# Batch norm after a matmul: six y blocks transposed raw by DMA, one store held to the end, and another warm-up on zeros

## The chip, the cores and the metric

One core of one Trainium2 chip runs the kernel. The metric is device time in microseconds (us) from launch to end; the profile's span, from the first to the last instruction, is somewhat shorter. The kernel before takes 207.84 us, the median of 8 runs (207.38 to 209.17).

## The reference

```python
y = np.matmul(x, weight)                     # x: 16 x 512 x 1024, weight: 1024 x 768, float32
mean = np.mean(y, axis=(0, 1), keepdims=True)
var = np.var(y, axis=(0, 1), keepdims=True)
y_norm = (y - mean) / np.sqrt(var + eps)
return (gamma * y_norm + beta).astype(np.float32)
```

So there are M = 8192 rows, K = 1024 and N = 768 columns. Every column is normalised with the mean and the variance of its 8192 values, so no value of a column can be stored before the whole column has been computed.

## The kernel before, in words

**Tiling.** The rows are cut into 16 chunks of 512 (c = 0 to 15), the columns into six tiles of 128 (nt = 0 to 5). x and weight are cast to bf16 by the loading DMAs, which POOL issues (L392, L383). DVE transposes x in 32 x 32 blocks (L421, L414) into `xT_sb`. Some chunks are copied once more into a plain layout `x_pl` (L530), on ACT during the loads; for chunks 11 to 15 the copies are made late, on POOL or DVE.

**Two ways to compute y.** The first two column tiles (256 columns) are computed with rows on the partitions for the first 14 chunks (L493) while x arrives; their sums lie in `sum1`, `sum2`, `sum3`. Column tiles 2 to 5 are computed with columns on the partitions (L558), so that statistics are one `bn_stats` on each bank (L694) and y is then cast to bf16 into `y_sb` tiles (L698). A y block is two chunks of one column tile: 128 columns by 1024 rows. After the last chunk of a column tile come its `bn_aggr` (L960), a root on ACT (L974) and the four small DVE operations of `affine` (L977 to L981), which give scale and shift.

**Ways out for a y block.** The block has to be transposed, normalised, widened to float32 and stored.
- `pe`: DVE normalises it (L1010), TensorE transposes it in eight 128 x 128 steps (L1028, through `turn_block`), put one by one between the long matmuls; ACT copies the bank out (L1171), SP stores (L1163).
- `xact`: DVE normalises it (L1010; for nt = 2 ACT does, L1007), SP issues a DMA transpose (L1181), ACT widens it (L1193), SP stores (L1163).
- raw: SP transposes the block by DMA before it is normalised (`raw_turn`, L1090). Scale and shift of that column tile are spread over 128 partitions by two float32 matmuls (`raw_spread`, L887), DVE multiplies (L1135), and one engine adds the shift (L1139), POOL before; SP stores (L1143). All raw transposes wait for the last load and are issued in one run ahead of the first store.

**Before**, raw blocks are c = 0 and 2 of nt = 2 and of nt = 4. The other blocks: nt = 2 has six `xact`, nt = 3 eight `xact`, nt = 4 one `xact` and five `pe`. Column tile 5 comes last: its final pieces (L736), their statistics (L743), `affine` (L1255 to L1257), normalisation (L1280), 64 transposes on TensorE (L1028), copies on ACT (L1293) and eleven stores by SP (L1296).

**Order.** Every engine runs its instructions in the order in which the builder emitted them (`seq`). That order comes from a planner (`arrange`): every task has a due time, a modelled duration for each engine that may do it, and the buffers it takes; the planner simulates the engines and picks. So a change of a mode moves other work too: an `x_pl` copy, which POOL and DVE may both do, goes to whichever the planner finds free. SP issues in order, so an instruction that waits holds everything behind it.

**The head.** While the first loads are under way, `wake` (L570) runs TensorE on a tile of zeros: 8 float32 matmuls of 512 columns (two passes each, 16 instructions, L574) and 22 bf16 matmuls of 128 columns (L577). Four tiny loads of weight values (L345, `touched`) are issued by SP at the start.

**Buffers.** There are 28 `y_sb` tiles (YB), which raw results and late `x_pl` copies share, and a float32 ring for results with room for six blocks, freed when a store has landed.

Of the kernel before, what the change touches and what calls it, by code (L numbers as in the profile page):

```python
# [227 lines left out]
def kernel(  # L228
# [9 lines left out]
    nc = tc.nc  # L238
    f32 = mybir.dt.float32
# [8 lines left out]
    P = 128  # L248
# [4 lines left out]
    C = M // CH  # L253
    QR = 256
    QPC = CH // QR
    JW = KQ // 64
    PIECES = ((0,QR),(QR,QR))
    WAKE = 8
    FILL = 2
    SMALL = 22  # L260
    TOUCH = 1
    EARLY = 4
    SHORT = 2
    GA = 2
    NA = GA * P
    GY = 2
    PAD = 54
    HELD = 0
    ASTAT = {2:tuple(range(4,16))}
    RC = C - 2  # L270
    XT, YB, SQ = C - EARLY, 28, 3
    ADDED = (0,6,16,28,40)
    PARTED, LATE, SINGLE = (4,5,7,8,9,10), (12,13,14,15,11), (2,3,6)
    MODE = {2:'xact',3:'xact',4:('pe',)*2+('xact',)*1+('pe',)*5}
    MODE = {nt: m if isinstance(m, tuple) else (m,) * (C // GY) for nt, m in MODE.items()}
    RAW, RAWADD, RAWDUE = {2:(0,2),4:(0,2)}, {2:'POOL',3:'POOL',4:'POOL'}, {2:14.0,3:8.0,4:8.0}
    RING = 3 * CH // 32 * KQ // 2
    ENG = {"ACT": nc.scalar, "DVE": nc.vector, "POOL": nc.gpsimd, "SP": nc.sync}

# [3 lines left out]
    singles = ctx.enter_context(tc.tile_pool(name="singles", bufs=1))  # L283
# [7 lines left out]
    def seq(bi):  # L291

        ins = bi.ins
        prev = last.get(ins.engine)
        if prev is not None:
            tc.add_manual_dep(
                ins, prev,
                mybir.DependencyInfo(mybir.DependencyClass.NoSync, mybir.DependencyReason.DATA),
                reason="order",
            )  # L300
        last[ins.engine] = ins.name
        return bi
# [12 lines left out]
    ones = singles.tile([P, 1], f32)  # L315
    seq(nc.vector.memset(ones, 1.0 / (RC * CH)))
    ident32 = singles.tile([P, P], f32)
    sum1 = singles.tile([P, 2 * NA], f32)
    sum2 = singles.tile([P, 2 * NA], f32)
    sum3 = singles.tile([P, 2 * NA], f32)  # L320
    for acc in (sum1, sum2, sum3):
        seq(nc.vector.memset(acc, 0.0))
    tot = singles.tile([P, 2, NA], f32)
    stats = singles.tile([P, (NT - GA) * C + PAD, 6], f32)
    fin = singles.tile([P, 9 + 6 * len(PIECES)], f32)
    psums = {nt: singles.tile([P, 2, C], f32, name=f"psums{nt}") for nt in ASTAT}
# [12 lines left out]
    warm = singles.tile([P, 1], f32)  # L339

    seq(nc.scalar.activation(warm, eps_sb, AF.Sqrt))
    touched = singles.tile([P, TOUCH], f32)
    first_rows = weight.rearrange("(i jw c e) n -> i jw c (e n)", i=4, jw=JW, e=2)
    for i in range(4):
        seq(nc.sync.dma_start(touched[32 * i:32 * i + 32], first_rows[i, 0, :, 0:TOUCH]))  # L345


    tasks, turns = [], {}
# [2 lines left out]
    def task(prio, engines, emit, deps=(), lock=False, **kw):  # L351
        t = Task(prio, engines, emit, deps, **kw)
        t.lock = lock
        tasks.append(t)
        return t
# [14 lines left out]
    STORE, XBAR = 1 / 350.0, 1.25  # L370
# [63 lines left out]
    for kind, n, *n1 in order:  # L434
# [13 lines left out]
        slot = Slot(rings, rows // 32 * KQ // 2)  # L448
# [7 lines left out]
        for i in range(rows // QR):  # L456
            c, q = divmod(m0 // QR + i, QPC)
            for j0, j1 in ((0, JW // 2), (JW // 2, JW)) if m0 < CH else ((0, JW),):
# [4 lines left out]
                    uses=[slot] if new else [slot, x_slot[c]], takes=[x_slot[c]] if new else [])  # L463
# [3 lines left out]
        if rows % QR:  # L467
            t0 = rows // QR * QR // 32
            m1 = m0 + 32 * t0
            c, q = divmod(m1 // QR, QPC)  # L470
# [139 lines left out]
    def col_unit(nt, c, jws, q0=0, q1=QPC):  # L610
        slot = bank_of.setdefault((nt, c), None) or Slot(banks)
        bank_of[nt, c] = slot
        first = jws[0] == 0 and q0 == 0
        xs = [plain[c][0][jw] for jw in jws] if c in plain else [x_slot[c]]
        kw = {"takes": [slot], "uses": xs} if first else {"uses": [slot] + xs}
        t = pe_task((1.728 if c in plain or c in SINGLE else 1.808) * len(jws) / JW * (q1 - q0) / QPC,
                    mm(nt, c, list(jws), slot, q0, q1),
                    waits(jws, c, q0, q1) + ([plain[c][1][jw] for jw in jws] if c in plain else []), (nt, c), **kw)
        if q1 - q0 == QPC:
            t.hosts = 4  # L620
        if jws[-1] == JW - 1 and q1 == QPC:
            col_stats(nt, c, slot, t)
        return t
# [60 lines left out]
    col_end = {}  # L684
# [91 lines left out]
    def merge(i):  # L776
        def emit(eng):
            acc = (sum1, sum2)[i]
            seq(ENG[eng].tensor_add(tot[:, i], acc[:, 0:NA], acc[:, NA:2 * NA]))
        return emit  # L780

    def more(h):
        def emit(eng):
            seq(nc.gpsimd.tensor_add(tot[:, 1], tot[:, 1], sum3[:, h * NA:(h + 1) * NA]))
        return emit

    ga_half = {}
# [46 lines left out]
    U = clock[0] - 30.0  # L834
# [14 lines left out]
    def sums_rows(eng):  # L849
        tot_ps = psum.tile([P, CH], f32, tag="b")  # L850
        aff["tot"] = tot_ps
        for i in range(2):
            for a in range(GA):
                j = i * GA + a
                seq(nc.tensor.matmul(  # L855
                    tot_ps[:, j:j + 1], tot[:, i, a * P:(a + 1) * P], ones,
                    start=True, stop=True, skip_group_check=True,
                ))

# [41 lines left out]
    U = S - 30.0  # L901
# [12 lines left out]
    def rows_out(c, s0, s1, k):  # L914
        due = S + 5.0 + 0.62 * k
        n = s1 - s0
        slot = Slot(rings, n * NA)

        def norm(eng):
            slot.o = piece(slot).rearrange("p (s n) -> p s n", n=NA)  # L920
            seq(nc.vector.tensor_mul(  # L921
                slot.o, y_row[c].y[:, s0:s1], aff[0][:, None, :].to_broadcast([P, n, NA])))

        def add(eng):
            row = sum1[:, 0:NA] if eng == "POOL" else aff[1]
            seq(ENG[eng].tensor_add(slot.o, slot.o, row[:, None, :].to_broadcast([P, n, NA])))  # L926

        def store(eng):
            m0 = c * CH
            seq(nc.sync.dma_start(  # L930
                out_flat[m0 + s0 * P:m0 + s1 * P, 0:NA].rearrange("(s p) n -> p s n", p=P), slot.o))

        keeps = [row_end[k][3] for k in row_end if k[0] == c]
        a = task(due, dve(0.3 * n), norm, [p0] + keeps, takes=[slot], uses=[y_row[c], a0_slot])
        b = task(due + 0.4, dve(0.3 * n) if k in ADDED else pool(0.59 * n), add, [a, p1 if k in ADDED else sh],
                 uses=[slot, a1_slot] if k in ADDED else [slot])
        task(due + 1.0, {"SP": (0.38, 0.4)}, store, [b], dma=n * NA * P * 4 / 1024 / 365.0 * 1.024,
             uses=[slot])

    k = 0  # L940
    for c in range(RC):
        for s0_, s1_ in ((0, 2), (2, 4)) if c < 2 else ((0, 4),):
            rows_out(c, s0_, s1_, k)
# [139 lines left out]
    def raw_turn(nt, c):  # L1083

        yslot, slot = y_of(nt, c), Slot(ys)

        def xbar(eng):
            r_sb = ypool.tile([P, GY * RT, P], bf16, tag="y")
            slot.r = r_sb
            bi = nc.sync.dma_start_transpose(slot.r, y(nt, c, GY))  # L1090
            if not gated:
                tc.add_manual_dep(
                    bi.ins, gate.ins.name,
                    mybir.DependencyInfo(mybir.DependencyClass.Sync, mybir.DependencyReason.DATA),
                    reason="behind the loads",
                )
                gated.append(bi)
            seq(bi)

        b = task(U, {"SP": (1.4, 1.4)}, xbar, [col_end[nt, c + i][1] for i in range(GY)] + [gate], dma=XBAR,  # L1100
                 takes=[slot], uses=[yslot])
        raw[nt, c] = slot, b

    raw, gated, raw_aff = {}, [], {}
    gate = last_loads[-1]
    for nt in RAW:
        for c in RAW[nt]:
            raw_turn(nt, c)

    def raw_spread(nt, fin_task):  # L1110
        bank = Slot(banks)
# [96 lines left out]
    for nt in range(GA, NT - 1):  # L1208
        if nt == NT - 2:
            for i, c in enumerate(LATE):  # L1210
                part_chunk(c, clock[0] + 0.0 + 4.0 * i, {"POOL": (1.1, 1.15), "DVE": (0.63, 0.7)},
                           i == 0, 4.0 / 4, [col_end[NT - 3, late[-1]][1]])
        for c in CHUNKS[nt]:
            for jws in halves if nt > GA or c > EARLY + 2 else [[jw] for jw in range(JW)]:
                col_unit(nt, c, jws)
        f = finish_tasks(nt)
        start = clock[0] + 3.0
        if nt in RAW:
            raw_spread(nt, f)
        for i in range(C // GY):  # L1220
            if (nt, GY * i) in raw:
                raw_block(nt, GY * i, start + STEP[nt] * i + RAWDUE[nt])
                continue
            if nt == NT - 2 and C // GY - HELD <= i:
                held.append((nt, GY * i, f))
                continue
            col_block(nt, GY * i, start + STEP[nt] * i, f)


    nt = NT - 1  # L1230
# [35 lines left out]
    for i, (hn, hc, hf) in enumerate(held):  # L1266
        b = col_block(hn, hc, E + 0.3 + 0.3 * i, hf)
# [3 lines left out]
    for c, r0, rows in ends:  # L1271
        due = E + 2.0 + 0.6 * c
        n = max(rows // CH, 1)
# [3 lines left out]
        for i in range(n):  # L1277
            def norm_part(eng, c=c + i, r0=r0, rows=min(rows, CH)):
# [5 lines left out]
                              uses=[y_of(nt, c + i)]))  # L1284
# [3 lines left out]
        slot = Slot(xts)  # L1288
# [6 lines left out]
        def store(eng, slot=slot, m0=m0, count=count):  # L1295
# [6 lines left out]
             uses=[slot])  # L1302
# [41 lines left out]
```

## Time and profile before

| what | us |
|---|---|
| median of 8 runs | 207.84 |
| the profiled execution | 207.81 |
| its span | 205.9 |
| around the span (207.81 less 205.9) | 1.9 |
| TensorE busy | 192.0 (93%) |
| DVE busy | 156.7 (76%) |
| ACT busy | 140.0 (68%) |
| POOL busy | 132.0 (64%) |

How to read it: the chain of work that ended last is followed back from the last instruction to whatever released each step. TensorE instructions are pipelined and overlap, so start-to-start times are read, not the sum of single durations. Loads fill the DMA engines up to 97 us and stores fill them from about 110 us on; between the two lies a stretch of about 10 us in which only the raw transposes run. A DMA queue's row shows when an instruction was issued, and for how long the issuing took, not when the data landed.

### The profile page before, as it was taken

The page shows a single profiled execution, that of the slowest core. Times are in us where ns is not written, and L with a number is a line of the kernel's source. Part 1 is how long each engine was busy: PE and PEld are TensorE (multiplying, and loading weights), DVE is VectorE, ACT ScalarE, POOL GpSimd, SP SyncE. Part 2 cuts the span into 40 slices and gives each one's busy share as a digit, 9 for nine tenths or more (in the row PEclk, how much of TensorE's full clock was granted, in tenths as well). Part 3 has the DMA queues.
Part 4 walks back from the last instruction along what each step waited for, and adds up shares of the span by engine and source line. Part 5 has one row for each costly group of instructions (what it writes and reads, how often), then busy time and mean ns, then how long its engine had stood idle before and what let it go on. Part 6 is the DMA issues. An engine that isn't in the chain of part 4 may idle for free.

```text
span 205.9 us, 3521 instructions
## 1 busy us (share of the span) xinstructions
PE 192.0 (93%) x1226; PEld 116.2 (56%) x1226; DVE 156.7 (76%) x238; ACT 140.0 (68%) x248; POOL 132.0 (64%) x148
## 2 busy tenths in 40 slices
PE   7999999999999999999999999999999999996900
PEld 3466564747488888777875444444444445553600
DVE  4220879998999999968989998888999648947900
ACT  2000560368989999998979767997476776866950
POOL 7877964877498999999304998599945440440000
PEclk9999999999999999999999999999999999999995
DMA  4999999999999999999696898999999999999898
GB/s 48 178 180 194 194 196 196 199 195 197 190 193 197 197 197 196 196 197 195 105 136 200 312 338 294 261 351 288 323 324 251 290 323 325 274 342 347 255 347 246
DMA packets 98497, 48.73 MB, mean 237 GB/s; under 512 B 24240, under 2 KB 97968, under 8 KB 98480
## 3 DMA queue, kind: packets, MB, share of 16 engines
q0 software_dynamic: 34688, 18.36, 65.1%
q1 hardware_dynamic: 63792, 30.16, 53.6%
q8 instruction: 9, 0.15, 0.3%
q14 instruction: 8, 0.07, 0.1%
HBM read 36.71 MB, written 25.17 MB: 300 GB/s over the span
## 4 chain that ended last, share of the span: by engine, by line
PE 82%; DMA 8%; ACT 3%; POOL 1%; issue 1%; DVE 1%; ACTq 0%; POOLq 0%
PE y_ps L558 52%; PE y_ps L493 23%; DMA ring<-in_x_dram 5%; PE y_ps L798 4%; ACT o_sb L1293 3%; DMA w_sb<-in_weight_dram 3%; PE o_ps L1028 2%; PE a_ps L887 1%; POOL ring L392 1%; PE y_ps L736 1%; PE o_ps L1058 0%; ACTq L1339 0%; PE tot_ps L855 0%; DVE fin L743 0%; ACT y_sb L746 0%
## 5 line engine op out<-in xcount | busy, mean ns | idle before, releaser
L558 PEld LDWEIGHTS <-w_sb 128*128 128x128 bf16 x512 | 49.6, 97 | 57.4
L558 PE MATMUL y_ps<-x_pl,w_sb 128*128 128x512 bf16 x264 | 61.3, 379 | 0.0
L558 PE MATMUL y_ps<-xT_sb,w_sb 128*128 128x512 bf16 (+1 forms) x248 | 55.9, 377 | 0.0
L392 POOL DMA_DIRECT2D ring<-in_x_dram x76 | 47.4, 628 | 12.5 <-DVE xT_sb L414 5.0
L493 PE MATMUL y_ps<-w_sb,xT_sb 128*128 128x256 bf16 x448 | 50.5, 273 | 0.3 <-DMA w_sb<-in_weight_dram 0.3
L493 PEld LDWEIGHTS <-xT_sb 128*128 128x128 bf16 x448 | 43.6, 98 | 7.8 <-issue 1.1
L421 DVE STREAM_TRANSPOSE xT_sb<-ring 128x1024 f32<-128x1024 f32 (+1 forms) x29 | 31.2, 1110 | 12.7 <-DMA ring<-in_x_dram 12.6
L694 DVE BATCH_NORM_STATS2 stats<-y_ps 128x6 f32<-128x512 f32 x46 | 30.7, 686 | 11.8 <-PE y_ps L558 11.6
L698 ACT CAST y_sb<-y_ps 128x512 bf16<-128x512 f32 x51 | 29.4, 590 | 14.2 <-DVE stats L694 11.6
L926 POOL TENSOR_TENSOR ring<-ring,sum 128x1024 f32<-128x1024 f32 (+1 forms) x11 | 23.8, 2184 | 14.8 <-DVE ring L921 14.7
L649 POOL TENSOR_TENSOR sum<-sum,sq_sb 128x512 f32<-128x512 f32 x21 | 26.9, 1281 | 2.9 <-ACT sq_sb L642 1.7
L642 ACT ACTIVATE sq_sb<-y_ps 128x512 f32<-128x512 f32 x28 | 16.2, 609 | 17.4 <-PE y_ps L493 17.0
L530 ACT COPY x_pl<-xT_sb 128x1024 bf16<-128x1024 bf16 x24 | 24.4, 1058 | 1.7 <-DVE xT_sb L421 1.7
L645 DVE TENSOR_TENSOR sum<-y_ps,sum 128x512 f32<-128x512 f32 x28 | 18.9, 674 | 8.5 <-ACT sq_sb L642 7.2
L655 ACT CAST y_sb<-y_ps 128x512 bf16<-128x512 f32 x28 | 16.1, 598 | 7.9 <-DVE sum L645 7.6
L530 POOL COPY x_pl<-xT_sb 128x1024 bf16<-128x1024 bf16 x15 | 16.0, 1106 | 8.0 <-DVE x_pl L530 5.2
L921 DVE TENSOR_TENSOR ring<-y_sb,a_ps 128x1024 f32<-128x1024 bf16 (+1 forms) x16 | 16.7, 1079 | 0.8 <-DMA out_dram<-ring 0.8
L1193 ACT CAST ring<-ring 128x1024 f32<-128x1024 bf16 x15 | 15.7, 1049 | 1.5 <-DMA ring<-y_sb 1.5
L1139 POOL TENSOR_TENSOR ring<-ring,sum 128x1024 f32<-128x1024 f32 x4 | 9.7, 2416 | 10.7 <-DVE ring L1135 10.7
L1028 PE MATMUL o_ps<-ident,y_sb 128*128 128x128 bf16 x104 | 14.2, 221 | 2.1 <-DVE y_sb L1280 2.0
L414 DVE STREAM_TRANSPOSE xT_sb<-ring 128x2048 bf16<-128x2048 bf16 x6 | 13.5, 2290 | 0.1
L574 PE MATMUL idle_ps<-idle_sb 128*128 128x512 f32 x20 | 11.2, 715 | 1.5 <-DVE idle_sb L314 1.5
(97 smaller groups left out, 155.2 us busy)
## 6 DMA issues: line engine op xcount, KB each, us to landing
out_dram<-ring SPq DMA_DIRECT2D x38, 512.0 KB, 3.8
ring<-in_x_dram POOLq DMA_DIRECT2D x52, 256.0 KB, 8.9
out_dram<-o_sb SPq DMA_DIRECT2D x6, 512.0 KB, 4.8
ring<-in_x_dram POOLq DMA_DIRECT2D x16, 128.0 KB, 5.3
out_dram<-ring SPq DMA_DIRECT2D x4, 256.0 KB, 3.0
w_sb<-in_weight_dram POOLq DMA_DIRECT2D x8, 96.0 KB, 4.9
w_sb<-in_weight_dram POOLq DMA_DIRECT2D x4, 192.0 KB, 5.6
ring<-in_x_dram POOLq DMA_DIRECT2D x4, 192.0 KB, 8.2
```

What stands on the lines that cost most here:

```text
L392: bi = seq(nc.gpsimd.dma_start(x_bf[32 * i:32 * i + 32], src[:, :, KQ * i:KQ * (i + 1)]))
L421: seq(nc.vector.transpose(dst, src[:, :, jw0:jw1]))
L493: seq(nc.tensor.matmul(y_ps[:, s], x_of(c, jw, e, t * P, (t + 1) * P), w_sb[:, jw, e, 0:NA], start=(s == 0 and jw == 0 and e == 0), stop=( ...
L530: seq(nc.scalar.copy(dst, pairs) if eng == "ACT" else ENG[eng].tensor_copy(dst, pairs))
L558: seq(nc.tensor.matmul(y_ps, w_sb[:, jw, e, nt * P:(nt + 1) * P], moving(c, jw, e, q0 * QR, q1 * QR, parted), start=(jw == 0 and e == 0 an ...
L645: seq(nc.vector.tensor_add(sum1, slot.tile[:, 0:n], sum1))
L649: seq(ENG[eng].tensor_add(acc, acc, state["sq"][:, 0:n]))
L694: seq(nc.vector.bn_stats(dst, slot.tile))
L698: seq(nc.scalar.copy(y(nt, c), slot.tile))
L921: seq(nc.vector.tensor_mul(slot.o, y_row[c].y[:, s0:s1], aff[0][:, None, :].to_broadcast([P, n, NA])))
L926: seq(ENG[eng].tensor_add(slot.o, slot.o, row[:, None, :].to_broadcast([P, n, NA])))
L1028: seq(nc.tensor.transpose(dst, src, ident))
```

## The change

- The raw blocks become six: c = 0 and 2 of nt = 2, 3 and 4. Their shift is added by DVE, not by POOL. `raw_spread` runs for nt = 3 too.
- nt = 3 has six `xact` blocks then (two fewer); nt = 4 has three `xact` (two more) and three `pe` (two fewer). One of the three `pe` blocks is held (HELD = 1): its transposes, its copy and its store come after the last long matmul, ahead of column tile 5's own.
- `wake` runs 5 float32 matmuls (10 instructions) and 72 small ones.
- The four tiny loads (`touched`) are left out.
- The row sums are folded in place in `sum1` and `sum2`, so the tile `tot` goes; the statistics tile is padded by less; there is one more `y_sb` tile (29).
- Of the 20 late `x_pl` copies POOL makes 19 and DVE one; before it was 15 and 5. This follows from the planner.

```diff
-    WAKE = 8
+    WAKE = 5
     FILL = 2
-    SMALL = 22
-    TOUCH = 1
+    SMALL = 72
...
-    PAD = 54
-    HELD = 0
+    PAD = 13
+    HELD = 1
...
-    XT, YB, SQ = C - EARLY, 28, 3
+    XT, YB, SQ = C - EARLY, 29, 3
...
-    MODE = {2:'xact',3:'xact',4:('pe',)*2+('xact',)*1+('pe',)*5}
+    MODE = {2:'xact',3:'xact',4:('pe',)*2+('xact',)*3+('pe',)*3}
...
-    RAW, RAWADD, RAWDUE = {2:(0,2),4:(0,2)}, {2:'POOL',3:'POOL',4:'POOL'}, {2:14.0,3:8.0,4:8.0}
+    RAWBEHIND = {}
+    RAW, RAWADD, RAWDUE = {2:(0,2),3:(0,2),4:(0,2)}, {2:'DVE',3:'DVE',4:'DVE'}, {2:14.0,3:0.0,4:0.0}
...
-    tot = singles.tile([P, 2, NA], f32)
...
-    touched = singles.tile([P, TOUCH], f32)
-    first_rows = weight.rearrange("(i jw c e) n -> i jw c (e n)", i=4, jw=JW, e=2)
-    for i in range(4):
-        seq(nc.sync.dma_start(touched[32 * i:32 * i + 32], first_rows[i, 0, :, 0:TOUCH]))
...
-            seq(ENG[eng].tensor_add(tot[:, i], acc[:, 0:NA], acc[:, NA:2 * NA]))
+            seq(ENG[eng].tensor_add(acc[:, 0:NA], acc[:, 0:NA], acc[:, NA:2 * NA]))
...
-            seq(nc.gpsimd.tensor_add(tot[:, 1], tot[:, 1], sum3[:, h * NA:(h + 1) * NA]))
+            seq(nc.gpsimd.tensor_add(sum2[:, 0:NA], sum2[:, 0:NA], sum3[:, h * NA:(h + 1) * NA]))
```

The rest of the diff only names things: `RAWBEHIND` is empty and adds no wait, and the loops over raw blocks give the same order for these blocks.

More of the change, by code (lines that the diff above doesn't have):

```diff
@@ L855, in sums_rows @@
                 seq(nc.tensor.matmul(
-                    tot_ps[:, j:j + 1], tot[:, i, a * P:(a + 1) * P], ones,
+                    tot_ps[:, j:j + 1], (sum1, sum2)[i][:, a * P:(a + 1) * P], ones,
                     start=True, stop=True, skip_group_check=True,
@@ L936, in rows_out @@
                  uses=[slot, a1_slot] if k in ADDED else [slot])
-        task(due + 1.0, {"SP": (0.38, 0.4)}, store, [b], dma=n * NA * P * 4 / 1024 / 365.0 * 1.024,
-             uses=[slot])
-    k = 0
+        row_stores.append(task(due + 1.0, {"SP": (0.38, 0.4)}, store, [b],
+                               dma=n * NA * P * 4 / 1024 / 365.0 * 1.024, uses=[slot]))
+    k, row_stores = 0, []
     for c in range(RC):
@@ L1098, in xbar @@
             seq(bi)
-        b = task(U, {"SP": (1.4, 1.4)}, xbar, [col_end[nt, c + i][1] for i in range(GY)] + [gate], dma=XBAR,
+        b = task(U, {"SP": (1.4, 1.4)}, xbar, [col_end[nt, c + i][1] for i in range(GY)] + [gate]
+                 + [row_stores[k] for k in RAWBEHIND.get((nt, c), ())], dma=XBAR,
                  takes=[slot], uses=[yslot])
@@ L1107 @@
         for c in RAW[nt]:
-            raw_turn(nt, c)
+            if c < EARLY:
+                raw_turn(nt, c)
     def raw_spread(nt, fin_task):
@@ L1215 @@
                 col_unit(nt, c, jws)
+        for c in RAW.get(nt, ()):
+            if c >= EARLY:
+                raw_turn(nt, c)
         f = finish_tasks(nt)
```

## The prediction

> **What bounds the kernel now.** I read the chain that ended last first, then its pieces in time.
>
> ```profile
> PE 82%; DMA 8%; ACT 3%; POOL 1%; issue 1%; DVE 1%; ACTq 0%; POOLq 0%
> ```
> ```profile
> 19.38 1.91 PE y_ps L493 x16
> ...
> 174.38 0.06 PE o_ps L1028
> 174.44 0.22 PE y_ps L558
> ...
> 186.49 1.83 PE y_ps L736 x16
> 188.34 0.44 DVE fin L743
> ```
> From 19.38 to 188.3 us TensorE never lets go of the end. Each transpose of a `pe` block (L1028) put between long matmuls costs it 0.055 us, the distance from 174.38 to 174.44. After 188.3 come statistics, then column tile 5's stores. What bounds those is in the stretches of 1 us (columns: busy us of PE, PEld, DVE, ACT, POOL, then clock, DMA share, GB/s).
>
> ```profile
> 190.00:191.00 1.00, 0.62 (x6) 0.31 (x7) 1.00 (x4) 0.34 (x2) 0.00 (x0) 1.00 1.01 307
> 191.00:192.00 1.00, 1.00 (x14) 0.71 (x15) 1.00 (x4) 0.96 (x4) 0.00 (x0) 1.00 0.09 29
> 192.00:193.00 1.00, 1.00 (x15) 0.71 (x14) 1.00 (x4) 1.00 (x2) 0.00 (x0) 1.00 0.87 260
> 203.00:204.00 1.00, 0.00 (x0) 0.00 (x0) 0.00 (x0) 0.00 (x0) 0.00 (x0) 0.50 1.15 347
> ```
> The DMA engines finish the older stores at about 190.8, stand still for 1 us, then move the eleven last stores at 347 GB/s until 204.45 (the next row has 156 GB/s, 0.45 of a full one). So the end is TensorE's end, a chain of small steps, and then bytes over bandwidth.
>
> **What the Trainium skill says.** "TensorE: Matmul & The Clock Gate", section "Wait — 56ns, not 53.3ns?": a warm 128-column matmul follows the last after 55.6 ns, a cold one after about 107 ns. The trace agrees on the first: 22 small ones from 10.63 to about 11.85 us, 0.055 each. "SBUF — State Buffer", section "Who interferes with whom": a DVE instruction in a two-port mode and a GpSimd instruction shut each other out. The trace agrees: the normalisation L1010 takes 0.54 us alone, 1.22 us at 148.66 beside POOL's copies. "DMA: Bandwidth & Descriptors", section "Latency and other measured facts": a DMA transpose (with a strided middle dimension) moved 261 GB/s. The trace is a little better: 284 to 295 GB/s where one runs, 340 to 360 in stores alone.
>
> **The head.**
> ```profile
> 10.63 1.39 PE L577 MATMUL idle_ps<-idle_sb 128*128 128x128 bf16 x22
> ...
> 19.38 1.91 PE L493 MATMUL y_ps<-w_sb,xT_sb 128*128 128x256 bf16 x16 [0.28 <-DMA w_sb<-in_weight_dram]
> ```
> Six long instructions go, at the warm distance of 0.43 us (their weight loads stand at 9.34, 9.77, 10.20): -2.57. Fifty small ones come: 50 x 0.055 = +2.75. The first real matmul moves from 11.86 to about 12.0. The cover: before 19.38 TensorE waits 0.28 us for the last piece of weight. Cost 0; without the cover +0.2. If the clock fell during the zeros, all 72 would take 0.107 (the skill's cold figure): +3.7 us, 3.5 behind the cover. The small ones before ran warm, so I take 0. The four tiny loads: SP does nothing else then; weights issued at 3.73 land 4.8 us later, 8.5 to 10.1, for use at 11.86, so 1.8 us of delay would be free, and no gain is in them, since x itself lands at 8.15. I take 0; up to +1 if weights come much later without them. In-place folding: the same operations, 0.
>
> **Six raw transposes.**
> ```profile
> 100.65 6.92 SPq L1090 DMA_TRANSPOSE r_sb<-y_sb  x4
> 109.61 0.41 SPq L930 DMA_DIRECT2D out_dram<-ring  x1
> ```
> The four were issued at 100.65, 102.08, 103.48 and 106.3, the third and fourth only when the first and second had landed (2.8 and 4.2 us later), since they take buffers that those free. With one more buffer the third needn't wait and the fourth waits for the first; the sixth waits for the third. At 1.4 us each I get an issue end of about 109.0 for six. The first store is ready at 109.58, so nothing moves. Behind SP stand all row stores; if each transpose cost its full 1.4 us, 107.57 + 2.8 = 110.4, +0.8 for them, while the DMA engines still have room (309 to 337 GB/s up to 125 us). I take 0.
>
> **DVE and POOL.**
> ```profile
> L1139 POOL TENSOR_TENSOR ring<-ring,sum 128x1024 f32<-128x1024 f32 x4 | 9.7, 2416 | 10.7 <-DVE ring L1135 10.7
> L1135 DVE TENSOR_TENSOR ring<-r_sb,a_ps 128x1024 f32<-128x1024 bf16 x4 | 4.8, 1209 | 0.1
> L926 DVE TENSOR_TENSOR ring<-ring,a_ps 128x1024 f32<-128x1024 f32 x3 | 3.6, 1214 | 0.1
> ```
> DVE gains six adds, 6 x 1.21 = 7.3, and two multiplies, 2.4; it loses two normalisations (0.67 each) and four copies (0.76 each): +5.3 us. POOL loses 9.7 and gains 4 x 1.1. DVE was busy for 27.0 of the 30 us from 130 to 160, so its list there runs late. Queued behind are `bn_stats`, and behind those ACT's casts, which free TensorE's banks. A raw pair now holds DVE for 4 x 1.21 = 4.8 us, under three chunks of 1.73 us; of eight banks one holds the spread, so seven are left, and TensorE should not run out.
>
> The tight place is nt = 3's new spread, which TensorE meets in order.
> ```profile
> 144.87 0.59 DVE L960 BATCH_NORM_AGGREGATE mv<-stats 128x2 f32<-128x96 f32 x1
> ...
> 147.57 1.05 DVE L981 SCALAR_TENSOR_TENSOR shift<-tmp,rstd,beta_sb 128x1 f32<-128x1 f32 x1
> ```
> Before, nt = 3's shift is ready at 148.6. Now two adds (2.42) stand ahead of the `bn_aggr`, less 0.81 us of idle time in that stretch, and one more `bn_stats` (0.69) before `affine`: up to 150.9, or 149.6 if POOL gets in the way less. By the built order TensorE comes to the spread 3.5 chunks into nt = 4. Chunk one's end lets `bn_stats` start at 145.86, so nt = 4 begins near 144.1 and the spread is due at 144.1 + 3.5 x 1.73 = 150.15. The stall is 0 to 0.8; I take 0.3.
>
> **TensorE's sum.** Between long matmuls stand 16 transposes instead of 40: -24 x 0.055 = -1.3. The new spread: +0.44 (the four passes at 127.88). The stall: +0.3. TensorE ends 0.57 earlier.
>
> **The tail.** Held block: normalised in DVE's gap before the last statistics; its eight transposes (0.44) fall into the 2 us in which TensorE waits for the last scale. Its copy (1.01, from L1171) stands on ACT behind the root and the last cast. Root ends at 189.38 - 0.57 = 188.8, cast 189.2, copy 190.2. Then column tile 5's first copy, ready at 190.1, waits 0.1. The held store is issued at about 190.25; data flowed 0.9 us after the issue at 191.06 before, so the stream begins at 191.15. It carries 4.19 MB (eleven stores) and 0.52 MB (held): 4.72 MB / 347 GB/s = 13.6 us, end 204.75 against 204.45: +0.3. The hole in the DMA engines is filled, TensorE is earlier, and the held store takes both back. The late transposes stay 15 (six, six, three instead of six, eight, one), so older stores should be done by 190.8 less the held one's 1.5 us; two transposes move to where stores are thick, and 1.9 us of new idle time would still be hidden.
>
> Sum against the profiled execution: 207.81 + 0.3 = 208.1; it is within 0.03 of the median, so the forecast is 208.1.
>
> **Rivals.**
> Slower, DVE late: the spread of nt = 3 and the banks wait for a DVE that runs further behind than I worked out. It decides from a shift ready 0.3 us after 150.15. For it: L980 and L981 took 0.87 and 1.05 us beside POOL's copies against 0.16 and 0.21 later, and POOL now copies without a break. Against: DVE has room again from 160. With 2 us of stall instead of 0.3: 209.8.
> Slower, stores late: nt = 4's three transposes and two slow raw stores keep the DMA engines beyond 191.15; each us adds one. At 1 us, 209.1.
> Slower, head: cold zeros or late weights, 209 to 211.6.
> Faster, the hole pays: no stall, and held data flow by 190.7, or the last stores ahead queue so well that no gap is left: TensorE's 0.87 comes through, about 207.0. Against: ACT's order puts the copy after the last cast.
>
> **How the numbers follow.** Main case 0.37 (207.6 to 208.6 of its own); DVE late 0.26; stores late 0.11; head 0.06; faster 0.20. About 0.3% (207.2 to 208.5) is what a measurement can tell from no change: 0.36 same, 0.20 faster, 0.44 slower, from the slower rivals and the main case's upper edge. The range runs from the faster case, 206.9, to the late DVE with both bounds of head and stores partly in, 210.2.
>
> **What would show it.** Right: L1028 before the last pieces x16; first store near 109.6; last piece's statistics near 187.8; held store issued near 190.3, then no hole at 191; DMA end about 0.3 later. Wrong: TensorE gaps ahead of L887 near 150, small zeros at 0.107, a first long stretch after 19.4, a hole that stays, or older stores still flowing at 191.

## The result

The changed kernel takes 210.2 us (median of 11 runs, 209.62 to 211.02), the kernel before on the same chip 208.23 (32 runs, 207.38 to 209.17). The ratio is 1.0092, 95% interval 1.0074 to 1.0110: slower by 1.9 us. That lies on the upper edge of the predicted range (206.9 to 210.2) and is no part of the case that the forecast of 208.1 stood on.

The profiled executions exaggerate: the one of after is its slowest run (211.02, span 209.0), the one of before (207.81) is among the fastest. So 3.2 us stand between the profiles, and 1.9 between the medians. Lines of the changed kernel are up to five lower than those of before (L553 was L558, L488 was L493, L1023 was L1028, L738 was L743); the last ones (L1280, L1293, L1296) are the same.

### The profile page after: what moved, and what is told of

Its sections match the earlier page's. It is cut to its first block, busy times and chain, and to the rows that moved or that the text cites. A ratio compares the mean times of both kernels' runs of the same rounds, so it can differ in the third digit from the quotient of the medians.

```text
span 209.0 us, 3574 instructions
## 1 busy us (share of the span) xinstructions
PE 193.0 (92%) x1258; PEld 117.7 (56%) x1258; DVE 160.1 (77%) x240; ACT 138.0 (66%) x247; POOL 126.0 (60%) x148
## 3 DMA queue, kind: packets, MB, share of 16 engines
q1 hardware_dynamic: 65712, 30.68, 53.1%
## 4 chain that ended last, share of the span: by engine, by line
PE 51%; DMA 19%; DVE 10%; POOL 6%; issue 5%; ACT 3%; ACTq 0%; DVEq 0%; POOLq 0%
PE y_ps L553 39%; DMA ring<-in_x_dram 16%; PE y_ps L488 5%; POOL ring L387 4%; DVE xT_sb L416 4%; PE y_ps L793 3%; ACT o_sb L1293 3%; DMA w_sb<-in_weight_dram 3%; DVE xT_sb L409 2%; POOL w_sb L378 2%; DVE sum L640 2%; PE a_ps L882 1%; PE y_ps L731 1%; DVE stats L689 1%; PE o_ps L1023 1%
## 5 line engine op out<-in xcount | busy, mean ns | idle before, releaser
L553 PEld LDWEIGHTS <-w_sb 128*128 128x128 bf16 x512 | 49.6, 97 | 57.0
L553 PE MATMUL y_ps<-x_pl,w_sb 128*128 128x512 bf16 x264 | 60.1, 379 | 0.0
L553 PE MATMUL y_ps<-xT_sb,w_sb 128*128 128x512 bf16 (+1 forms) x248 | 55.9, 377 | 0.0
L488 PE MATMUL y_ps<-w_sb,xT_sb 128*128 128x256 bf16 x448 | 50.7, 273 | 0.5 <-DMA w_sb<-in_weight_dram 0.3
L488 PEld LDWEIGHTS <-xT_sb 128*128 128x128 bf16 x448 | 43.5, 98 | 8.6 <-issue 1.7
L525 POOL COPY x_pl<-xT_sb 128x1024 bf16<-128x1024 bf16 x19 | 19.6, 1074 | 10.0 <-PE y_ps L553 9.8
L569 PE MATMUL idle_ps<-idle_sb 128*128 128x512 f32 x14 | 9.2, 819 | 1.5 <-DVE idle_sb L314 1.5
L1023 PE MATMUL o_ps<-ident,y_sb 128*128 128x128 bf16 x88 | 8.9, 221 | 1.6 <-DVE y_sb L1280 1.6
L698 ACT ACTIVATE y_sb<-y_ps 128x512 bf16<-128x512 f32 x12 | 7.2, 603 | 3.0 <-PE y_ps L553 3.0
```

Source lines behind the costliest of these rows:

```text
L488: seq(nc.tensor.matmul(y_ps[:, s], x_of(c, jw, e, t * P, (t + 1) * P), w_sb[:, jw, e, 0:NA], start=(s == 0 and jw == 0 and e == 0), stop=( ...
L525: seq(nc.scalar.copy(dst, pairs) if eng == "ACT" else ENG[eng].tensor_copy(dst, pairs))
L553: seq(nc.tensor.matmul(y_ps, w_sb[:, jw, e, nt * P:(nt + 1) * P], moving(c, jw, e, q0 * QR, q1 * QR, parted), start=(jw == 0 and e == 0 an ...
```

## The profile after, stretch by stretch

First the head and the body, from the timeline of the changed kernel (start, length in us, engine, line, what, and in brackets the idle time ahead and what ended it):

```profile
8.69 4.18 PE L572 MATMUL idle_ps<-idle_sb 128*128 128x128 bf16 x72
20.24 0.92 PE L488 MATMUL y_ps<-w_sb,xT_sb 128*128 128x256 bf16 x7 [0.29 <-DMA w_sb<-in_weight_dram]
...
102.27 8.33 SPq L1085 DMA_TRANSPOSE r_sb<-y_sb  x6
111.19 0.41 SPq L925 DMA_DIRECT2D out_dram<-ring  x1
...
189.17 0.43 DVE L738 BATCH_NORM_STATS2 fin<-y_ps 128x6 f32<-128x256 f32 x1 [0.48 <-PE y_ps L731]
190.38 1.01 ACT L1168 CAST ring<-o_ps 128x1024 f32<-128x1024 bf16 x1
191.90 0.52 SPq L1296 DMA_DIRECT2D out_dram<-o_sb  x1
```

The last weight comes 0.86 us later than before (20.24 against 19.38). Six raw transposes are issued in 8.33 us, and the first store follows 0.6 us behind them (2.0 us behind the four before). While x still arrives, TensorE falls back further, to 1.58 us behind the kernel before at 97 to 150 us; after that it makes up, and its last statistics stand 0.83 us later than before. So TensorE explains 0.83 of the 3.2 us between the profiles, and the rest came after it.

The waits of TensorE in the whole changed kernel (us in total, times, longest):

```profile
PE o_ps L1023 <- DVE y_sb L1280: 1.6, 1, 1.6
PE idle_ps L569 <- DVE idle_sb L314: 1.5, 1, 1.5
PE y_ps L488 <- DMA w_sb<-in_weight_dram: 0.3, 1, 0.3
```

There is no wait at the new spread of nt = 3 (L882), which the chain has without a break:

```profile
151.72 0.45 PE a_ps L882 x4
152.17 22.45 PE y_ps L553 x104
```

Now the tail of the changed kernel, in stretches of 1 us (PE, PEld, DVE, ACT, POOL busy, clock, DMA share, GB/s):

```profile
190.00:191.00 1.00, 0.00 (x0) 0.00 (x0) 0.76 (x5) 1.00 (x3) 0.00 (x0) 1.00 1.16 349
191.00:192.00 1.00, 0.78 (x8) 0.45 (x8) 1.00 (x5) 0.89 (x3) 0.00 (x0) 1.00 0.60 182
192.00:193.00 1.00, 1.00 (x15) 0.68 (x12) 1.00 (x5) 0.99 (x3) 0.00 (x0) 1.00 0.72 220
...
205.00:206.00 1.00, 0.00 (x0) 0.00 (x0) 0.00 (x0) 0.00 (x0) 0.00 (x0) 0.50 1.12 337
206.00:207.00 1.00, 0.00 (x0) 0.00 (x0) 0.00 (x0) 0.00 (x0) 0.00 (x0) 0.50 0.09 25
207.00:208.00 1.00, 0.00 (x0) 0.00 (x0) 0.00 (x0) 0.00 (x0) 0.00 (x0) 0.50 0.05 14
```

Two things are to be seen. The hole at 191 is half filled (182 and 220 GB/s, where before had 29 and 260). And the stream does not end as it did: it falls from 337 to 25 GB/s at 206, and goes on at that rate until 207.65. One sixteenth of 347 is 21.7 GB/s: **one of the 16 DMA engines is still at work when the others are done**. After 206.1 there are 65 rows of 512 bytes left, one after the other, over 1.5 us. In the kernel before the stream ends within one stretch (347, 156, 0).

What put one engine behind? The page's third part has a queue that the prediction did not look at. The first line is from the page of before, the second from that of after (packets, MB, share of the engines):

```profile
q8 instruction: 9, 0.15, 0.3%
```
```profile
q8 instruction: 10, 0.16, 0.3%
```

Each packet is 16,384 bytes and keeps one DMA engine for 0.9 to 1.7 us. The trace has their times (start in us, in brackets the length of the last one):

```
before  ... 103.91  128.78  153.45  178.86 (1.28)
after   ... 101.99  118.01  145.77  175.22  195.47 (1.25)
```

The Trainium skill says what they are ("Runtime: NRT & Kernel Launch", section "Instruction fetch mechanics"): an engine's instructions are fetched by DMA in blocks of 16 KiB, 256 instructions each, and the cost is "mostly hidden". The trace agrees with the size, and in its number of instructions too: between the first and the last fetch it records 2,000 TensorE instructions before and 2,315 after, 250 and 257 for each fetch. Fifty more small matmuls with a weight load each, less the six long ones and theirs, make TensorE's stream longer by some 90 instructions, so every block is fetched earlier (the first at 15.86 us, before at 22.82), and a tenth comes in time to fall into the last stores.

**Theory A:** the fetch at 195.47 takes 1.25 us of one DMA engine in a stretch in which all of them are full to the end, so that engine's share of the last store ends that much later. **Theory B:** the later head and the busier DVE cost the time, and the fetch is only there as well. **Theory C:** the four tiny loads had done something for the head.

## The experiments

The experiments were timed in five rounds against the kernel before on the same chip. Only ratios are compared between chips.

| run | us | ratio to before | interval | last fetch |
|---|---|---|---|---|
| changed kernel | 210.2 | 1.0092 | 1.0074 to 1.0110 | 195.5 |
| b_wake | 210.0 | 1.0076 | 1.0050 to 1.0102 | 194.2 |
| b_wide | 208.85 | 1.0016 | 0.9994 to 1.0037 | 177.9 |
| a_wide | 208.82 | 0.9999 | 0.9978 to 1.0021 | 178.2 |
| a_touch | 212.4 | 1.0212 | 1.0171 to 1.0253 | 196.1 |
| b_notouch | 211.06 | 1.0129 | 1.0100 to 1.0158 | 180.6 |
| a_head | 212.34 | 1.0190 | 1.0158 to 1.0223 | 185.7 |
| a_touch2 | 210.76 | 1.0096 | 1.0061 to 1.0132 | 195.8 |
| b_notouch2 | 208.89 | 1.0009 | 0.9991 to 1.0027 | 180.3 |
| a_off64 | 211.61 | 1.0152 | 1.0122 to 1.0183 | 179.1 |
| a_off256 | 208.43 | 1.0005 | 0.9988 to 1.0023 | 178.0 |
| a_held0 | 208.84 | 1.0022 | 1.0008 to 1.0036 | 178.7 |
| a_early | 217.82 | 1.0463 | 1.0433 to 1.0494 | 194.3 |

### The warm-up alone: b_wake

The kernel before with the changed kernel's zeros, nothing else.

```diff
-    WAKE = 8
+    WAKE = 5
-    SMALL = 22
+    SMALL = 72
```

> The kernel before with the other warm-up alone: 5 long and 72 small matmuls on zeros. My prediction says 0 (first real matmul +0.16, hidden behind the weights). If the other warm-up is what makes the first real matmul late (12.71 against 11.86) and that reaches the end: about 0.9 us slower, 209.1.

Measured: 1.0076. The warm-up alone brings nearly the whole loss, without any of the work on raw blocks. Its tail, in the same columns as above:

```profile
204.00:205.00 1.00, 0.00 (x0) 0.00 (x0) 0.00 (x0) 0.00 (x0) 0.00 (x0) 0.50 1.15 346
205.00:206.00 1.00, 0.00 (x0) 0.00 (x0) 0.00 (x0) 0.00 (x0) 0.00 (x0) 0.50 0.68 204
206.00:207.00 1.00, 0.00 (x0) 0.00 (x0) 0.00 (x0) 0.00 (x0) 0.00 (x0) 0.50 0.07 19
```

The lone engine is there too (19 GB/s until 206.9). But this run has the later start of the real work as well, so it does not yet part A from B.

### The same zeros in half as many instructions: a_wide and b_wide

36 small matmuls of 256 columns take the place of 72 of 128: a_wide in the changed kernel, b_wide in the kernel before with 5 long zero matmuls.

```diff
-    SMALL = 72
+    SMALL = 36
...
-            small = idle_sb[:, 0:P // 2].bitcast(bf16)
+            small = idle_sb[:, 0:P].bitcast(bf16)
...
-                seq(nc.tensor.matmul(idle_ps[:, 0:P], small, small, start=True, stop=True))
+                seq(nc.tensor.matmul(idle_ps[:, 0:2 * P], small[:, 0:P], small, start=True, stop=True))
```

> The changed kernel with 36 small zero matmuls of 256 columns in place of 72 of 128: the same time on zeros, 36 matmuls and 36 weight loads fewer in TensorE's stream. Theory A (an instruction fetch of 16 KB falls into the saturated last stores because TensorE's stream is longer): nine fetches, none after 190 us, no lone DMA engine at the end, 1.3 to 1.7 us less than the changed kernel: about 208.6 (208.3 to 209.0). Theory B (the later clock and the spread cost the time, the fetch is hidden): 210.2, as the changed kernel.

> The kernel before with the changed kernel's 5 long zero matmuls and 36 small ones of 256 columns. Theory A: the warm-up itself costs only its later start, up to 0.9 us, of which the load-bound phase swallows part, and no fetch falls into the tail: 208.3 to 208.9. Theory B (the head costs the time through a later first matmul): 210.0, as with 72 of 128 columns.

Measured: 0.9999 and 1.0016. The timeline of a_wide shows that the time on zeros is the same (4.09 us against 4.18, the first real matmul at 12.63 against 12.71):

```profile
8.70 4.09 PE L572 MATMUL idle_ps<-idle_sb 128*128 128x256 bf16 x36
12.63 0.60 PE L488 MATMUL y_ps<-w_sb,xT_sb 128*128 128x256 bf16 x4
```

Its page again has nine fetches, and its tail ends almost at once (the last 25 rows take 0.5 us; in the changed kernel one engine was alone for 1.6 us):

```profile
q8 instruction: 9, 0.15, 0.3%
```
```profile
191.00:192.00 1.00, 1.00 (x13) 0.80 (x12) 1.00 (x4) 1.00 (x2) 0.00 (x0) 0.76 1.13 335
192.00:193.00 1.00, 1.00 (x12) 1.00 (x11) 1.00 (x5) 0.90 (x2) 0.00 (x0) 0.50 1.15 347
...
204.00:205.00 1.00, 0.00 (x0) 0.00 (x0) 0.00 (x0) 0.00 (x0) 0.00 (x0) 0.50 0.93 277
205.00:206.00 1.00, 0.00 (x0) 0.00 (x0) 0.00 (x0) 0.00 (x0) 0.00 (x0) 0.50 0.03 8
```

Against the changed kernel the ratio falls by 0.0093 (half-width 0.0028), 1.9 us, and the intervals do not touch: within that width it is the whole loss. These two profiles differ ahead of the tail as well (last statistics at 189.17 and 187.94; all of that gap was there by 98 us, when the last of x had arrived), so they alone would not show where the time went. The pair on the body of before is cleaner. There the ratio falls by 0.0060 (b_wake to b_wide, half-width 0.0034), 1.25 us; the first matmul after the last weight starts almost alike (19.80 and 19.96), and so do the last statistics (189.21 and 189.29); only the tail differs. Theory A holds, on two bodies; theory B is left with at most 0.2 to 0.4% (the upper ends of the two intervals).

The trace does not name the engine that a packet ran on. That the late engine is the one that fetched is inferred: it is there with the fetch and not without it, and the bytes agree. In the three stretches from 195 us the stores of the changed kernel move 335, 328 and 342 KB where a full stretch has 347, some 36 KB less, and 65 rows, 33 KB, are what the lone engine still has to move after 206.1.

### The tiny loads, and what moved with them: a_touch, b_notouch, a_head, a_touch2, b_notouch2

At first the four loads were put back into the changed kernel with their tile (a_touch), taken from the kernel before with their tile (b_notouch), and put back together with the old warm-up (a_head).

```diff
+    touched = singles.tile([P, TOUCH], f32)
+    first_rows = weight.rearrange("(i jw c e) n -> i jw c (e n)", i=4, jw=JW, e=2)
+    for i in range(4):
+        seq(nc.sync.dma_start(touched[32 * i:32 * i + 32], first_rows[i, 0, :, 0:TOUCH]))
```

> The changed kernel with the four tiny weight loads put back and nothing else. In the profiled runs the last weight piece landed at 20.11 us in the changed kernel against 19.25 before. If the missing tiny loads make the weights land late, it goes back to about 19.3 and the time falls by about 0.9 us, to 209.3. If they are idle work, as I predicted, the time stays at 210.2.

> The kernel before without the four tiny loads. If they matter: about 0.9 us slower than before, 209.1, and the last weight lands near 20.1. If they don't: 208.2, as before.

> The changed kernel with the head of before: tiny loads and 8 long, 22 small matmuls; so the blocks, the held store and the engines of the adds are all that is changed. If the loss is in the head, about +0.3 us against before, 208.5 (the tail as predicted). If it is in the blocks and the tail, it keeps the whole +1.9, 210.1.

Measured: 1.0212, 1.0129, 1.0190. None of the theories gave that: putting the loads back cost 2.5 us against the changed kernel, and taking them away cost 2.7 us against the kernel before. The stretch from 203 us, first in b_notouch, then in b_notouch2, which leaves out the loads and keeps the tile:

```profile
203.00:204.00 1.00, 0.00 (x0) 0.00 (x0) 0.00 (x0) 0.00 (x0) 0.00 (x0) 0.50 1.01 271
```
```profile
203.00:204.00 1.00, 0.00 (x0) 0.00 (x0) 0.00 (x0) 0.00 (x0) 0.00 (x0) 0.50 1.15 347
```

In this stretch the last stores move at 275, 271 and 299 GB/s in a_touch, b_notouch and a_head, at 346 or 347 where no tile was added or taken. The tile of 4 bytes moves everything allocated after it by 32 bytes, `o_sb` among it. So these three runs say nothing on the loads. (In a_head the rate explains only a part of its 4.0 us: it has 346 GB/s up to 201 us and 286 after, and a hole ahead of that, 43 and 139 GB/s from 186 to 188, whose cause stays open.) The pair of runs that keeps every tile in place does say something; in a_touch2 the loads land in an unused column of the statistics' padding:

```diff
+    for i in range(4):
+        seq(nc.sync.dma_start(stats[32 * i:32 * i + 32, (NT - GA) * C + PAD - 1, 0:1], first_rows[i, 0, :, 0:1]))
```

> The changed kernel with the four tiny loads of weight put back, landing in an unused column of the statistics' padding, so that no tile moves. If the tiny loads do nothing (as predicted): 210.2, fetch near 195.5 and the lone engine still there. If the last weight comes later without them and that is what delays the head: 209.3 to 209.6, with the first long stretch at 19.4 and not 20.2.

> The kernel before without the four tiny loads, but with their tile kept, so that no tile moves. If the loads do nothing: 208.3, last stores at 347 GB/s as before. The run that left out tile and loads gave 211.06 with last stores at some 288 GB/s; if it was the loads and not the addresses, this one gives 211 too.

Measured: 1.0096 against 1.0092 without them, and 1.0009 against 1. In a_touch2 the work after the last weight starts at 21.01, so the loads do not bring it earlier, and one engine is alone at the end for 1.7 us, as in the changed kernel (its fetch is at 195.81). Theory C falls.

### Where a tile starts: a_off64 and a_off256

Into a_wide an unused tile is put ahead of the pools: `offset = singles.tile([P, 16], f32)`, 64 bytes a partition, or `[P, 64]`, 256 bytes. In the built programs the pool of `o_sb` starts at byte 66,560 before, 63,488 after (both multiples of 512), 63,552 in a_off64, 63,744 in a_off256.

> The run with 36 wide zero matmuls, with an unused tile of 64 bytes a partition put in ahead of the tile pools, so that the tiles from which the last stores read start 64 bytes past a multiple of 256. If the start has to be a multiple of 256 bytes[...], the last stores move at 288 GB/s and not 347, and 4.7 MB take 2.7 us longer: some 211.3, ratio 1.013. If only multiples of 64 matter (the earlier slow runs stood at an odd multiple of 32): as without the tile, ratio 1.000.

> The same with an unused tile of 256 bytes a partition: the tiles start at a multiple of 256, but not of 512. If 256 is what matters: 347 GB/s, ratio 1.000 (0.997 to 1.003). If whole rows of 512 bytes must lie on multiples of 512: some 288 GB/s and ratio 1.013.

Measured: 1.0152 and 1.0005. The same stretch of a_off64 and of a_off256:

```profile
203.00:204.00 1.00, 0.00 (x0) 0.00 (x0) 0.00 (x0) 0.00 (x0) 0.00 (x0) 0.50 0.93 277
```
```profile
203.00:204.00 1.00, 0.00 (x0) 0.00 (x0) 0.00 (x0) 0.00 (x0) 0.00 (x0) 0.50 1.15 345
```

So a multiple of 256 is enough, one of 64 is not. The direction agrees with the Trainium skill ("DMA: Bandwidth & Descriptors", section "How a descriptor splits into AXI transactions"): a read is cut at multiples of 256 bytes, so that a row of 512 that starts beside one takes three pieces instead of two. The size does not. Counted in the page's beats of 32 bytes it would be 18 instead of 16 here, an estimate of 347 x 16 / 18 = 308 GB/s; 17 in a_touch and a_head (32 bytes past a multiple of 256), 327; and 23 in b_notouch (224 past), 241. Counted in pieces it would be 347 x 2 / 3 = 231 in all of them, an estimate too. Measured are 284 GB/s from 196 to 206 us in a_off64, a_touch and b_notouch alike. That the three are alike fits a count of pieces better than one of beats, but neither gives 284, and what sets it is not shown.

Nor does the start alone decide: a_head has the same start as a_touch, and since only some 2.1 MB are left after 201 us, about half of its last stores (4.19 MB) must have moved at 346. What let them is open. At 284 instead of 347 GB/s the 4.19 MB of the last stores take 2.7 us more (the held store reads `ring`, which no tile here moved); 3.2 (1.0152 less 0.9999, half-width 0.8) were measured.

For the change this means that the smaller statistics padding (13 rows for 54), together with the tiles that went, leaves `o_sb` on a multiple of 512. That cost nothing, but only because it came out so.

### The held block: a_held0

a_wide with `HELD = 0`.

> The changed kernel with 36 wide zero matmuls (no fetch in the tail) and HELD = 0: the third pe block goes out between the long matmuls and not after them. If the held store pays for itself by filling the hole ahead of the last stores: without it the hole at 191 is back, the older stores carry 1.5 us more, and the time is within 0.3% of the run with the held block, ratio 1.000 (0.997 to 1.003). If the held store costs what TensorE had gained (the prediction's step): TensorE ends 0.4 us later, the last stores flow 1.5 us less long, about 0.5 to 1 us faster than the run with the held block: ratio to before 0.995 to 0.998.

Measured: 1.0022 against 0.9999 with the held block; the intervals overlap, and no gain is in it. Its tail:

```profile
190.00:191.00 1.00, 0.74 (x8) 0.43 (x8) 1.00 (x5) 0.46 (x2) 0.00 (x0) 1.00 1.14 347
191.00:192.00 1.00, 1.00 (x16) 0.70 (x13) 1.00 (x5) 0.99 (x3) 0.00 (x0) 1.00 1.17 355
192.00:193.00 1.00, 1.00 (x15) 0.68 (x12) 1.00 (x5) 1.00 (x2) 0.00 (x0) 1.00 1.14 332
```

Both expectations missed the middle: no hole comes back although nothing is held, since the older stores flow right on into the last ones. The data end at 205.32 us with `HELD = 0` and at 205.37 with the held block. In these two profiles the DMA engines are full without a break from before 187 to the end, so it does not matter in which order the same bytes go. That does not hold for every execution of this body: the changed kernel's own profile, of its longest run, has half a hole at 191.

### An earlier fetch: a_early

```diff
-    WAKE = 5
+    WAKE = 2
-    SMALL = 72
+    SMALL = 132
```

> The changed kernel with 2 long and 132 small zero matmuls: TensorE's stream is some 108 instructions longer still, so that the last fetch comes earlier, near 189 to 191 us, at or ahead of the hole in the DMA engines. If the fetch costs only where no slack follows on its engine: ten fetches, no lone engine at the end, 1.3 us less than the changed kernel, less up to 0.6 for the later start of the real matmuls: 208.7 to 209.5. If the number of fetches or of instructions is what costs: 210.2 or more.

Measured: 217.82. The edit did more than was meant: `wake` adds the small ones whenever its count equals WAKE, and the second warm-up has FILL = 2 as count. So 264 of them ran, and the last statistics stand at 197.57, 8.4 us later than in the changed kernel. The total can't be used. Its profile still bears on the question: eleven fetches, the last at 194.34, six us ahead of the first of the last stores (200.29), and no lone engine at the end:

```profile
200.00:201.00 1.00, 0.96 (x13) 0.66 (x12) 1.00 (x5) 0.99 (x3) 0.00 (x0) 0.91 0.33 100
...
213.00:214.00 1.00, 0.00 (x0) 0.00 (x0) 0.00 (x0) 0.00 (x0) 0.00 (x0) 0.50 1.15 346
214.00:215.00 1.00, 0.00 (x0) 0.00 (x0) 0.00 (x0) 0.00 (x0) 0.00 (x0) 0.50 0.46 136
215.00:216.00 1.00, 0.00 (x0) 0.00 (x0) 0.00 (x0) 0.00 (x0) 0.00 (x0) 0.50 0.00 0
```

A hole (100 GB/s at 200) lies between the fetch and the last stores, in which an engine that is behind can catch up. This fits "where the fetch falls decides, not how many there are", in one profile and without a time of its own. a_touch points the same way: its fetch at 196.12 lies amid the last stores, but these fill the engines less (a DMA share of 0.96 at 284 GB/s, against 1.15 at 347), and the stream ends without a lone engine (289, 205 and 1 GB/s from 207 us).

## Why the prediction was right in part, and where it failed

**The time on record, 208.1, is that of the change without the fetch**: a_wide, with all of the change but the number of zero matmuls, stands at 0.9999. What failed is the step on the head, "Fifty small ones come: 50 x 0.055 = +2.75 ... Cost 0". It priced the fifty matmuls as time on TensorE, which was right, and put at nothing that their instructions have to be fetched by the same DMA engines that bound the tail. That term measures 1.9 us in the changed kernel and 1.25 on the body of before. No rival had it: that 210.2 still lies in the range is luck, since the range reached so far only for other mishaps (a late DVE above all, which did not come).

- **Head, time.** Predicted first real matmul 12.0; measured 12.71 in the changed kernel, and 11.25 to 12.78 in the nine profiles with five long zero matmuls (11.13 to 11.92 in the four with eight). The time at which the long ones turn fast differs between executions: their distance falls from 0.85 to 0.43 us at 5.9 us before, at some 7 us in the changed kernel, at 4.9 in b_wake. The small ones ran warm (4.02 us for 72, 0.056 each). The work after the last weight, for which a start after 19.4 was to be a sign of being wrong, began at 20.24; but over all profiles it begins between 19.18 and 21.01 with the new zeros and between 19.27 and 20.05 with the old ones, so that sign tells little. In b_wide the new zeros, in wide form, cost 0.16% (-0.06 to 0.37). For this part a cost of 0 was right to about 0.4%.
- **Tiny loads, 0.** Right (b_notouch2, a_touch2).
- **Six raw transposes, 0.** Right, to the tenth: TensorE stands 1.58 us later at that time, so the issue end of 110.60 is 109.0 and the first store 109.6 on the clock of before.
- **DVE +5.3, POOL -5.3.** The page of after, to be held against 156.7 and 132.0 before:

```profile
PE 193.0 (92%) x1258; PEld 117.7 (56%) x1258; DVE 160.1 (77%) x240; ACT 138.0 (66%) x247; POOL 126.0 (60%) x148
```

  DVE +3.4, POOL -6.0: DVE was oversized by 1.9. The stall at nt = 3's spread, taken at 0.3, was 0 in this profile: less the 1.58 us, TensorE comes to it at 150.14 (predicted 150.15) and the shift is ready at 149.74 (predicted 149.6 to 150.9). So the rival "DVE late" did not come, by some 0.4 us.
- **TensorE ends 0.57 earlier.** From 150 us to the last statistics the distance to before goes from +1.58 to +0.83: 0.75 earlier. With the stall taken out the sum had been 0.87. Nearly right.
- **The tail gives it back.** That it does was right: a_wide's last statistics come 0.40 us earlier than before, its data end at 205.37 (before 204.69, in one of its fastest executions), and its median equals that of before to 0.2%. The reason was not right: it is not the held store, since without it the end is the same. What has grown is the queue of SP's DMAs, from 30.16 to 30.68 MB by the pages: two more blocks transposed by DMA, 0.52 MB, 1.5 us at 347 GB/s. That these bytes keep the older stores from ending before the last ones is read from the profiles and no experiment shows it.
- **Rivals.** "Stores late" named the right resource and the wrong user. Of "head", the zeros stayed warm. "The hole pays" fell: in a_wide there is no hole and no stall, and still no gain.

No run beats the kernel before; a_wide and a_off256 equal it.

## What to carry to other kernels

An instruction costs its time on the engine and its place in a stream that is itself fetched by DMA: when instructions are added or dropped anywhere, look at the times of the instruction packets, and see that none falls where the DMA engines are full until the end. The same work in fewer, wider instructions is the cheap way out. And before an experiment adds or drops a tile, keep the start of every later tile that DMA reads, or two effects are measured as one.

## What of the hardware was not expected

- One fetch of 16 KB keeps one of 16 DMA engines for 1.25 us and, in a full tail, puts the end of the data off by about as much (one engine alone for 1.3 to 1.7 us in the profiles, 1.25 to 1.9 us in the medians).
- Stores in rows of 512 bytes, read by DMA from SBUF at starts 32, 64 or 224 bytes past a multiple of 256, moved at 284 GB/s, at multiples of 256 at 347; in one run (a_head) about half of them moved at full rate all the same.
- Six DMA transposes of raw blocks were issued in 8.33 us where four had taken 6.92 before: all six came at 1.4 us each. One more buffer goes with it, as predicted; the buffer was not changed alone.
